# Two output projections, recast from half-by-half products into seven quadrant products

## The chip, the cores and the metric

The kernel runs on one core of a Trainium2 chip. Its time is the device time of one execution in microseconds. The change is timed against the kernel before it.

## The reference, cut to what matters

The program is a trunk of two layers over x of 1024 tokens by 1024 channels, in float32. The first layer is a gated DeltaNet (8 heads, keys of 128, values of 256, chunks of 64 in the reference), the second a sliding-window attention with sinks (32 query heads of 64, 4 key heads, window 128). Each layer ends in the same way: a gated output o of 1024 x 2048 is multiplied by a weight of 2048 x 1024 and added to the residual stream.

```
x = x + gated_deltanet_mixer(rms_norm(x, a_norm), ...)   # ... o (1024, 2048) @ a_w_out (2048, 1024)
k_band, v_band = shared_kv(x, kv_norm, w_kv, k_gain)
x = x + swa_sink_mixer(rms_norm(x, b_norm), ...)         # ... o (1024, 2048) @ b_w_out (2048, 1024)
```

These two matrix products are what the change is about.

## The kernel before

Float32 accuracy is had from TensorE with pairs: every operand is kept as a rounded high part (hi, oh, hh) and the rest (lo, ol, hl), and a product is three matmuls, high by high, high by low, low by high, accumulated in PSUM.

**Weights.** `weights()` is a generator that yields all weight pieces of the program in the order of use, each of 128 partitions x 1024 columns. `fetch()` takes the next piece: `weight_load` allocates a `wraw` tile (a pool of two buffers) and issues the load on SP's queue; then the high part is cast (on GpSimd where no gain is applied, L148; on ScalarE behind a multiplication by the gain on GpSimd, L150 and L151) and VectorE subtracts it for the low part (L152). `take()` hands out the oldest prepared weight and fetches until `depth` weights are ready. The pools from which hi and lo come rotate in `wpools`: in the first projection three buffers with a depth of 2, in the second two buffers with a depth of 1.

**The DeltaNet layer.** `layer_a` works head by head. `interleave` alternates the recurrence of one head (`head_delta`, a chain of small matmuls, VectorE and ScalarE steps) with the input projections of the next head (`head_in`, `head_z`, through `gemm_ct`, L175 to L179, 512 columns a matmul); TensorE's order is written out by that alternation and kept as it is, while the other engines' instructions are ordered by a scheduler. `head_out` writes the gated, transposed output of a head to `ogT` in DRAM (16 tiles of 128 channels x 1024 tokens). Head 7 comes last, and with it the z products of the two `late` heads.

**The attention layer.** `layer_b` does the same with `b_attend` (32 heads in 8 groups) and the q and z projections (`b_q`, `b_z`); its gated output goes to `og2` in DRAM.

**A projection.** `out_proj` goes over two halves of 512 tokens. In each half it goes over two pairs of 256 output columns; in each pair over four groups k4 of 512 input channels and the two column blocks b, with one weight tile each ([4, 256] per partition); for each weight tile over four blocks of 128 tokens and four channel blocks kk, three matmuls of 256 columns each (L913 to L915). Four PSUM tiles are accumulated over all of k4 and then added to the residual tiles `xo` (L919) and stored. The tokens' operand is held whole for a half: four pairs oh, ol of [128, 4, 512], loaded by `og_load` (a load of 512 KB on ScalarE's queue, a cast on ScalarE at L888, a subtraction on VectorE at L889, twice a pair). The second half's pairs replace the first's during the last column pair of the first half. After a half, `finish` normalizes the tokens and transposes them into `hT` for what follows (first projection only); `later` and `tick` place those transposes between matmuls.

Of the kernel before, what the change touches and what calls it, by code (L numbers as in the profile page):

```python
# [18 lines left out]
P = 128  # L19
# [45 lines left out]
class Kernel:  # L65
# [72 lines left out]
    def weight(self, src, shape, gain=None):  # L138
# [8 lines left out]
        if gain is None:  # L147
# [7 lines left out]
    def fetch(self):  # L155

        nxt = next(self.sources, None)
        if nxt is not None:
            self.ready.append(self.weight(*nxt))

# [90 lines left out]
    def layer_a(self):  # L251
        nc, tc, I = self.nc, self.tc, self.I
        with ExitStack() as ctx:
# [76 lines left out]
            for h in range(AH):  # L330
                cur = self.cur
                back = []
# [4 lines left out]
                if h + 1 == AH:  # L337
                    back += [self.head_z(i, None) for i in late]
                    self.first = self.og_tiles(self.dl0, "kq", "vt")
                    self.og_load(self.ogT, 0, 0, self.first, self.raws)  # L340
# [550 lines left out]
    def out_proj(self, og, resid, cur, tiles, raws, px, acc, dst, finish):  # L891


        nc = self.nc
        for half in range(2):
            xs, nxt = [], []
            for cp in range(2):
                cs = slice(cp * 512, cp * 512 + 512)
                ps = [acc.tile([P, 2, 256], F32, name="acc") for _ in range(4)]
                for k4 in range(4):  # L900
                    oh, ol = cur[k4]
                    for b in range(2):
                        hi, lo = self.take()
                        if cp == 0 and (k4, b) == (2, 0):
                            self.flush()
                            for c in range(4):
                                xs.append(px.tile([P, D], F32, name="xo", bufs=4))
                                nc.sync.dma_start(xs[c], resid[half * 4 + c])
                        for c in range(4):
                            ts = slice(c * P, c * P + P)  # L910
                            po = ps[c][:, b, :]
                            for kk in range(4):
                                nc.tensor.matmul(po, oh[:, kk, ts], hi[:, kk, :], start=(k4 + kk + b == 0), stop=False)  # L913
                                nc.tensor.matmul(po, oh[:, kk, ts], lo[:, kk, :], start=False, stop=False)  # L914
                                nc.tensor.matmul(po, ol[:, kk, ts], hi[:, kk, :], start=False, stop=(k4 + kk + b == 7))  # L915
                                if kk % 2:
                                    self.tick()
                            if (k4, b) == (3, 1):
                                nc.vector.tensor_tensor(out=xs[c][:, cs], in0=ps[c].rearrange("p b c -> p (b c)"),  # L919
                                                        in1=xs[c][:, cs], op=ALU.add)  # L920
                                nc.sync.dma_start(dst[half * 4 + c][:, cs], xs[c][:, cs])
                    if half == 0 and cp == 1:
                        nxt.append(tiles(k4))
                        self.og_load(og, 1, k4, nxt[-1], raws)
            cur = nxt
            finish(half, xs)
# [97 lines left out]
    def layer_b(self, last):  # L1024
# [4 lines left out]
        X = self.groups  # L1029
        X[0].keys, steps = self.key_stack(0)  # L1030
# [14 lines left out]
        def ahead():  # L1045
            for k4 in range(3):
                self.og_load(self.og2, 0, k4, last[k4], raws)
                yield 0.0
# [3 lines left out]
        self.og_load(self.og2, 0, 3, last[3], raws)  # L1052
# [198 lines left out]
    def run(self):  # L1251
        nc, tc, I = self.nc, self.tc, self.I
        with ExitStack() as ctx:
# [12 lines left out]
            self.late = (5, 6)  # L1266
            self.win = I["a_w_in"].rearrange("o (k p) c -> p (o k) c", p=P)
# [4 lines left out]
            with ExitStack() as c1:  # L1272
                hp = pool(c1, "hT")
                self.hT = self.hT_tiles(hp)
                with ExitStack() as c2:
# [23 lines left out]
                    def tiles(k4):  # L1299
                        return self.og_tiles(po, f"oh{k4}", f"ol{k4}") if k4 else self.og_tiles(self.dl0, "kq", "vt")  # L1300

                    cur = [self.first]
                    for k4 in range(1, 4):
                        cur.append(tiles(k4))
                        self.og_load(self.ogT, 0, k4, cur[-1], self.raws)
                    self.out_proj(self.ogT, xv, cur, tiles, self.raws, px, acc, x1d, finish)
# [21 lines left out]
                with ExitStack() as c2:  # L1328
                    px = pool(c2, "px2", 2)
                    self.out_proj(self.og2, x1d, last, lambda k4: last[k4],  # L1330
                                  lambda j: px.tile([P, 2, 512], F32, name="oraw"), px, pool(c2, "acc2", 6, space=PSUM), ov,
                                  lambda half, xs: None)

    def weights(self):
# [17 lines left out]
        for _ in range(2):  # L1352
            for c in (0, 2):
                for k in range(4):
                    for b in range(2):
                        yield four(rows("a_w_out"), k, c + b, None)
# [10 lines left out]
        for _ in range(2):  # L1367
            for c in (0, 2):
                for k in range(4):
                    for b in range(2):  # L1370
# [25 lines left out]
```

## Time and profile before

| | |
|---|---|
| time, median of 3 executions | 1904.08 us (1901.43 to 1906.32) |
| the profiled execution | 1903.49 us, its span 1901.7 us |
| TensorE, VectorE, ScalarE, GpSimd busy | 1831.0, 1232.2, 813.6, 517.1 us |
| DeltaNet layer after its start, to its last head's end | 100 to 903 us of the span |
| first output projection | 906.06 to 1095.27 us |
| keys and values, attention layer | 1095 to 1713 us |
| second output projection | 1713.34 to 1897.75 us |

A time here is that of one profiled execution; positions are counted from its first instruction. Records of TensorE's matmuls overlap, since one begins before the record of the one before it has ended; so the spacing of their starts tells the pace, and the duration of one does not. "PEld" is the load of the stationary operand.

### The profile page before, as it was taken

How to read it: one execution, taken by the hardware profiler on the slowest of the kernel's cores; microseconds unless marked ns; L12 is line 12 of the kernel's file. 1: busy time of each engine (PE TensorE's matmuls, PEld its weight loads, DVE VectorE, ACT ScalarE, POOL GpSimd, SP SyncE). 2: the span in 40 equal slices, each digit the busy share in tenths (PEclk: the TensorE clock that was granted, in tenths of full speed). 3: DMA queues.
4: the chain of work that ended last, by engine and by line, in shares of the span. 5: the costliest groups of instructions: out<-in, count | busy, mean ns of one | idle time of the engine just before them, and what ended most of it. 6: DMA issues, size and time to landing. Idle time of an engine off the chain costs nothing.

```text
span 1901.7 us, 33658 instructions
## 1 busy us (share of the span) xinstructions
PE 1831.0 (96%) x13186; PEld 1566.8 (82%) x13186; DVE 1232.2 (65%) x2868; ACT 813.6 (43%) x1948; POOL 517.1 (27%) x545
## 2 busy tenths in 40 slices
PE   6999999999999998999999999999999999999999
PEld 6677777787878776778999998888788788879999
DVE  6677766768585878765445266787786686753432
ACT  6446353535334353523112043557756656771100
POOL 0332222323232223220211222333433333321111
PEclk9999999999999999999999999999999999999999
DMA  4611111111111111122654321111201111226542
GB/s 148 148 37 39 55 35 56 34 56 45 34 57 34 57 34 57 34 84 95 233 181 153 112 89 45 45 30 51 67 29 51 56 40 51 73 73 196 185 172 80
DMA packets 151267, 149.72 MB, mean 79 GB/s; under 512 B 7242, under 2 KB 124484, under 8 KB 151108
## 3 DMA queue, kind: packets, MB, share of 16 engines
q1 hardware_dynamic: 140768, 130.40, 22.0%
q10 hardware_dynamic: 10340, 17.16, 2.8%
q8 instruction: 104, 1.70, 0.4%
q14 instruction: 55, 0.45, 0.1%
HBM read 116.05 MB, written 31.49 MB: 78 GB/s over the span
## 4 chain that ended last, share of the span: by engine, by line
PE 59%; DVE 20%; issue 8%; ACT 6%; POOL 5%; DMA 1%; SPq 0%; POOLq 0%; ACTq 0%; DVEq 0%
PE mm L177 6%; PE mm L175 6%; PE mm L179 6%; PE acc L914 6%; PE acc L913 6%; PE acc L915 6%; DVE acc L489 4%; PE mm L965 3%; PE mm L967 3%; PE mm L966 3%; DVE wlo L152 2%; ACT lsb L1176 2%; PE pv L1207 1%; POOL acc L486 1%; PE sc L796 1%
## 5 line engine op out<-in xcount | busy, mean ns | idle before, releaser
L175 PE MATMUL mm<-hh,whi 128*128 128x512 f32 (+1 forms) x1040 | 427.2, 411 | 2.3 <-ACT hh L241 2.2
L177 PE MATMUL mm<-hl,whi 128*128 128x512 f32 (+1 forms) x1040 | 417.5, 401 | 1.5 <-DVE hl L242 1.5
L179 PE MATMUL mm<-hh,wlo 128*128 128x512 f32 (+1 forms) x1040 | 415.2, 399 | 0.0
L152 DVE TENSOR_TENSOR wlo<-wraw,whi 128x1024 fp32r<-128x1024 f32 x146 | 184.2, 1262 | 245.7 <-POOL whi L148 219.4
L148 POOL TENSOR_SCALAR whi<-wraw 128x1024 fp32r<-128x1024 f32 x110 | 120.3, 1094 | 504.9 <-PE acc L915 246.4
L175 PEld LDWEIGHTS mm<-hh,whi 128*128 128x128 f32 x1040 | 197.6, 190 | 37.5 <-issue 5.0
L179 PEld LDWEIGHTS mm<-hh,wlo 128*128 128x128 f32 x1040 | 197.2, 190 | 36.2 <-issue 4.2
L177 PEld LDWEIGHTS mm<-hl,whi 128*128 128x128 f32 x1040 | 197.6, 190 | 34.4 <-issue 4.2
L965 PE MATMUL mm<-whi,hh 128*128 128x256 f32 x608 | 180.1, 296 | 0.0
L489 DVE SCALAR_TENSOR_TENSOR acc<-u,cw,acc 128x512 f32<-128x512 f32 x192 | 163.3, 853 | 23.9 <-POOL acc L486 21.8
L967 PE MATMUL mm<-whi,hl 128*128 128x256 f32 x608 | 171.9, 283 | 0.0
L966 PE MATMUL mm<-wlo,hh 128*128 128x256 f32 x608 | 171.8, 283 | 0.0
L913 PE MATMUL acc<-whi,hh 128*128 128x256 f32 x512 | 145.0, 283 | 0.0
L914 PE MATMUL acc<-wlo,hh 128*128 128x256 f32 x512 | 144.9, 283 | 0.0
L915 PE MATMUL acc<-whi,hl 128*128 128x256 f32 x512 | 144.9, 283 | 0.0
L1176 ACT ACTIVATE lsb<-lsb,nm 128x128 f32<-128x128 f32 x256 | 99.8, 392 | 64.2 <-DVE se L1172 54.9
L965 PEld LDWEIGHTS mm<-whi,hh 128*128 128x128 f32 x608 | 115.8, 190 | 11.0 <-issue 10.8
L966 PEld LDWEIGHTS mm<-wlo,hh 128*128 128x128 f32 x608 | 115.9, 191 | 0.2
L967 PEld LDWEIGHTS mm<-whi,hl 128*128 128x128 f32 x608 | 115.6, 190 | 0.0
L486 POOL TENSOR_SCALAR acc<-u,cw 128x512 f32<-128x512 f32 x64 | 63.0, 984 | 181.2 <-ACT u L482 166.8
L1180 POOL TENSOR_TENSOR lsb<-lsb,den 128x512 f32<-128x512 f32 x64 | 68.5, 1070 | 152.6 <-ACT pT L1190 51.5
L914 PE MATMUL acc<-wlo,oh 128*128 128x256 f32 x384 | 108.6, 283 | 0.0
(354 smaller groups left out, 4285.1 us busy)
## 6 DMA issues: line engine op xcount, KB each, us to landing
wraw<-in_a_w_in SPq DMA_DIRECT2D x48, 512.0 KB, 3.9
wraw<-in_a_w_out SPq DMA_DIRECT2D x32, 512.0 KB, 3.7
wraw<-in_b_w_in SPq DMA_DIRECT2D x32, 512.0 KB, 4.0
wraw<-in_b_w_out SPq DMA_DIRECT2D x32, 512.0 KB, 3.7
og<-zs SPq DMA_DIRECT2D x32, 256.0 KB, 2.0
ogT<-zs SPq DMA_DIRECT2D x24, 256.0 KB, 2.1
btab<-lt SPq DMA_DIRECT2D x1, 4096.0 KB, 24.1
dm<-gd SPq DMA_DIRECT2D x8, 512.0 KB, 3.6
```

Of the source, the lines that this page charges most:

```text
L152: nc.vector.tensor_tensor(out=lo, in0=raw, in1=self.f32(hi), op=ALU.subtract)
L175: nc.tensor.matmul(ps, hi[:, k, :], hh[:, k, :], start=(k == 0), stop=False)
L177: nc.tensor.matmul(ps, hi[:, k, :], hl[:, k, :], start=False, stop=False)
L179: nc.tensor.matmul(ps, lo[:, k, :], hh[:, k, :], start=False, stop=(k == KT - 1))
L489: nc.vector.scalar_tensor_tensor(out=acc, in0=u[:, t:t + 512], scalar=cw[:, t, blk:blk + 1], in1=acc, op0=ALU.mult, op1=ALU.add)
L913: nc.tensor.matmul(po, oh[:, kk, ts], hi[:, kk, :], start=(k4 + kk + b == 0), stop=False)
L914: nc.tensor.matmul(po, oh[:, kk, ts], lo[:, kk, :], start=False, stop=False)
L915: nc.tensor.matmul(po, ol[:, kk, ts], hi[:, kk, :], start=False, stop=(k4 + kk + b == 7))
L965: nc.tensor.matmul(ps, hh[:, k, ts], hi[:, k % 4, :], start=(k == 0), stop=False)
L966: nc.tensor.matmul(ps, hh[:, k, ts], lo[:, k % 4, :], start=False, stop=False)
L967: nc.tensor.matmul(ps, hl[:, k, ts], hi[:, k % 4, :], start=False, stop=(k == KT - 1))
L1176: nc.scalar.activation(out=L[:, e, :], in_=L[:, e, :], func=AF.Exp, bias=nm[:, e:e + 1], accum_out=den[:, e:e + 1])
```

## The change

With the two halves of the tokens, of the input channels and of the output columns, each projection is a product of 2 x 2 quadrants (o: tokens by channels; w: channels by columns). Instead of eight quadrant products it makes seven, after Strassen: each is the product of a quadrant, or a sum or difference of two, of o, with a quadrant or such a sum of w, and its result is added to or subtracted from one or two quadrants of the output. `PRODUCTS` lists them as (terms of o), (terms of w), (where the result goes, with sign).

- Five of the seven need a sum of two weight quadrants. `product_sums` forms these ahead of time, piece by piece (40 pieces of 128 x 512 a projection): two loads into a `wraw` tile, an addition on GpSimd, a store to `sums` in DRAM. One step is done at each `fetch()` (`self.side`): for the first projection in the DeltaNet layer from head 0 on, with what is left done ahead of head 7; for the second from the start of the attention layer, and on into the projection as far as needed.
- A weight tile is now [2, 512] per partition; its high part is cast on ScalarE (`second=True`).
- The tokens' operand passes through a ring of three pairs (first projection) or four (second), each for half a product (four channel blocks). `load` brings a quadrant into `whole` buffers (parts of hT that are free by then, in the first projection; three tiles `room` in the second), forms the sum on GpSimd where there are two terms, and splits it.
- All eight residual tiles are held from the start and loaded in quarters during the first two products. At the end of each product its PSUM tiles are added to or subtracted from them on VectorE; a quarter is stored when its last term has come. `finish` comes for the first half of the tokens after the sixth product, for the second half after the seventh.

```diff
+    PRODUCTS = (
+        (((1, 0, 0),), ((1, 0, 1), (-1, 1, 1)), ((0, 1, 1), (1, 1, 1))),
+        (((1, 1, 0), (-1, 0, 0)), ((1, 0, 0), (1, 0, 1)), ((1, 1, 1),)),
+        (((1, 1, 0), (1, 1, 1)), ((1, 0, 0),), ((1, 0, 1), (1, 1, -1))),
+        (((1, 0, 0), (1, 1, 1)), ((1, 0, 0), (1, 1, 1)), ((0, 0, 1), (1, 1, 1))),
+        (((1, 0, 0), (1, 0, 1)), ((1, 1, 1),), ((0, 0, -1), (0, 1, 1))),
+        (((1, 1, 1),), ((1, 1, 0), (-1, 0, 0)), ((1, 0, 1), (0, 0, 1))),
+        (((1, 0, 1), (-1, 1, 1)), ((1, 1, 0), (1, 1, 1)), ((0, 0, 1),)),
+    )
...
     def weight(self, src, shape, gain=None, second=False):
...
+        if second:
+            nc.scalar.copy(out=hi, in_=raw)
+        elif gain is None:
...
     def fetch(self):
...
             self.ready.append(self.weight(*nxt))
+            if self.side is not None:
+                next(self.side, None)
...
+    def product_sums(self, w, sums):
...
+            for i in range(8):
+                t = self.wraw.tile([P, 2, 512], F32, name="wraw")
+                for j, (_, k, c) in enumerate(terms):
+                    nc.sync.dma_start(t[:, j, :], w[:, 8 * k + i, 512 * c:512 * c + 512])
+                nc.gpsimd.tensor_tensor(out=t[:, 0, :], in0=t[:, 0, :], in1=t[:, 1, :],
+                                        op=ALU.add if terms[1][0] > 0 else ALU.subtract)
+                yield
+                nc.sync.dma_start(sums[n, i], t[:, 0, :])
...
+    def out_proj(self, og, resid, ring, ready, raws, whole, px, acc, dst, finish):
...
+        def load(u):
+            terms = self.PRODUCTS[u // 2][0]
+            oh, ol = ring[u % len(ring)]
+            src = [quadrant(t, k, u % 2) for _, t, k in terms]
+            for j in range(2):
+                js = slice(2 * j, 2 * j + 2)
+                if len(src) == 1:
+                    raw = src[0][:, js, :]
+                else:
+                    raw = raws(j)
+                    nc.gpsimd.tensor_tensor(out=raw, in0=src[0][:, js, :], in1=src[1][:, js, :],
+                                            op=ALU.add if terms[1][0] > 0 else ALU.subtract)
+                nc.scalar.copy(out=oh[:, js, :], in_=raw)
+                nc.vector.tensor_tensor(out=ol[:, js, :], in0=raw, in1=self.f32(oh[:, js, :]), op=ALU.subtract)
...
+        for m, (_, _, sinks) in enumerate(self.PRODUCTS):
+            ps = [acc.tile([P, 512], F32, name="acc") for _ in range(4)]
+            for j in range(4):
+                hi, lo = self.take()
+                if (m, j) == (0, 3):
+                    self.flush()
+                if m < 2 and j in (1, 2):
+                    for c in range(4):
+                        tc.keep_in_program_order(nc.sync.dma_start(xs[j - 1][c][:, 512 * (1 - m):1024 - 512 * m],
+                                                                   resid[(2 - j) * 4 + c][:, 512 * (1 - m):1024 - 512 * m]))
+                oh, ol = ring[(2 * m + j // 2) % len(ring)]
+                for c in range(4):
+                    ts = slice(c * P, c * P + P)
+                    for kk in range(2):
+                        k = 2 * (j % 2) + kk
+                        nc.tensor.matmul(ps[c], oh[:, k, ts], hi[:, kk, :], start=(j + kk == 0), stop=False)
+                        nc.tensor.matmul(ps[c], oh[:, k, ts], lo[:, kk, :], start=False, stop=False)
+                        nc.tensor.matmul(ps[c], ol[:, k, ts], hi[:, kk, :], start=False, stop=(j == 3 and kk == 1))
+                        self.tick()
+                    if j == 3:
+                        for t, q, sign in sinks:
+                            x = xs[t][c][:, 512 * q:512 * q + 512]
...
+                            if left[t, q] == 1:
+                                nc.sync.dma_start(dst[(1 - t) * 4 + c][:, 512 * q:512 * q + 512], x)
+                if j % 2 and 2 * m + j // 2 + len(ring) < 14:
+                    load(2 * m + j // 2 + len(ring))
...
+                if h == 0:
+                    self.side = self.product_sums(self.rows("a_w_out"), self.sums[0])
+                elif h + 1 == AH:
+                    for _ in self.side:
+                        pass
+                    self.side = None
```

## Rows read from the trace of the kernel before

**Rows 1.** The page: span, busy time of each engine, TensorE's granted clock in 40 slices.
```profile
span 1901.7 us, 33658 instructions
PE 1831.0 (96%) x13186; PEld 1566.8 (82%) x13186; DVE 1232.2 (65%) x2868; ACT 813.6 (43%) x1948; POOL 517.1 (27%) x545
...
PEclk9999999999999999999999999999999999999999
```

**Rows 2.** Busy time in four stages: layer, projection, layer, projection.
```profile
core 0: us, PE busy (x) PEld busy (x) DVE busy (x) ACT busy (x) POOL busy (x), PEclk, DMA share, GB/s
100.00:903.36 803.36, 767.98 (x5375) 609.29 (x5373) 582.95 (x1104) 339.94 (x794) 217.74 (x231) 0.99 0.16 49
906.06:1095.27 189.21, 188.04 (x1571) 187.83 (x1570) 79.52 (x90) 25.91 (x35) 39.70 (x34) 1.00 0.52 171
1120.00:1712.00 592.00, 580.19 (x4050) 493.86 (x4048) 420.29 (x1412) 364.10 (x968) 200.26 (x218) 0.99 0.16 51
1713.34:1897.75 184.41, 184.41 (x1538) 184.36 (x1536) 65.34 (x60) 13.95 (x15) 31.80 (x30) 1.00 0.48 160
```

**Rows 3.** What TensorE waited for, over the span, longest in total first.
```profile
PE sc L810 <- DVE lh L799: 8.3, 10, 1.9
...
PE tp L1186 <- POOL lsb L1180: 6.1, 5, 2.7
...
PE acc L914 <- DVE wlo L152: 1.2, 1, 1.2
```

**Rows 4.** Timeline of TensorE: first and last of the second projection's 1536 matmuls.
```profile
1713.34 0.38 PE L913 MATMUL acc<-whi,hh 128*128 128x256 f32 x1
...
1897.63 0.28 PE L915 MATMUL acc<-whi,hl 128*128 128x256 f32 x1
```

**Rows 5.** Timeline of TensorE: first and last of 23 consecutive 512-column matmuls.
```profile
898.10 0.39 PE L177 MATMUL mm<-hl,whi 128*128 128x512 f32 x1
...
903.09 0.39 PE L179 MATMUL mm<-hh,wlo 128*128 128x512 f32 x1
```

**Rows 6.** Groups of instructions by form, second projection (the cast on ScalarE: first).
```profile
L151 ACT CAST whi<-wraw 128x1024 fp32r<-128x1024 f32 x2 | 2.1, 1047 | 63.9 <-PE acc L915 63.9
...
L152 DVE TENSOR_TENSOR wlo<-wraw,whi 128x1024 fp32r<-128x1024 f32 x30 | 36.7, 1224 | 95.8 <-POOL whi L148 95.8
L148 POOL TENSOR_SCALAR whi<-wraw 128x1024 fp32r<-128x1024 f32 x30 | 31.8, 1060 | 148.0 <-PE acc L915 133.9 <-DMA wraw<-in_b_w_out 14.1
L889 DVE TENSOR_TENSOR hl<-oraw,hh 128x1024 fp32r<-128x1024 f32 x8 | 11.9, 1526 | 10.9 <-ACT hh L888 10.9
L919 DVE TENSOR_TENSOR xo<-acc,xo 128x512 f32<-128x512 f32 x15 | 10.1, 690 | 10.8 <-PE acc L915 10.8
```

**Rows 7.** DMA issues by line: count, size, median us from issue to landing.
```profile
wraw<-in_b_w_out SPq DMA_DIRECT2D x32, 512.0 KB, 3.7
og<-zs SPq DMA_DIRECT2D x32, 256.0 KB, 2.0
...
xo<-x1d SPq DMA_DIRECT2D x8, 512.0 KB, 7.2
```

**Rows 8.** Busy time in a stretch at the first projection's start (columns as above).
```profile
920.00:925.00 5.00, 5.00 (x44) 5.00 (x43) 2.76 (x3) 0.96 (x1) 2.10 (x1) 1.00 1.06 384
```

**Rows 9.** Timeline at the change of half, second projection: start, us, engine.
```profile
1770.39 2.00 ACT L888 CAST hh<-oraw 128x1024 fp32r<-128x1024 f32 x2 [46.02 <-PE acc L914]
...
1771.46 3.07 DVE L889 TENSOR_TENSOR hl<-oraw,hh 128x1024 fp32r<-128x1024 f32 x2 [3.64 <-ACT hh L888]
1774.46 1.21 DVE L152 TENSOR_TENSOR wlo<-wraw,whi 128x1024 fp32r<-128x1024 f32 x1
```

**Rows 10.** GpSimd's groups in the attention layer; two instructions of the first projection.
```profile
L1180 POOL TENSOR_TENSOR lsb<-lsb,den 128x512 f32<-128x512 f32 x64 | 68.5, 1070 | 152.6 <-ACT pT L1190 51.5 <-DVE den L1179 49.2 <-ACT zs L1108 19.1
L150 POOL TENSOR_TENSOR wraw<-wraw,gcolb 128x1024 f32<-128x1024 f32 x32 | 67.4, 2109 | 80.2 <-DMA wraw<-in_b_w_in 46.3 <-DVE sskb L981 7.3 <-DVE rkbt L118 5.2
...
908.97 2.06 DVE L889 TENSOR_TENSOR ol<-kt,oh 128x1024 fp32r<-128x1024 f32 x1
...
921.03 2.10 POOL L148 TENSOR_SCALAR whi<-wraw 128x1024 fp32r<-128x1024 f32 x1 [6.82 <-DMA wraw<-in_a_w_out]
```

More of the change, by code (lines that the diff above doesn't have):

```diff
@@ L136, in weight_first, with weight @@
         self.ready.append((hi, lo))
-    def weight(self, src, shape, gain=None):
+    def weight(self, src, shape, gain=None, second=False):
         nc = self.nc
@@ L889, in og_load @@
             nc.vector.tensor_tensor(out=ol[:, js, :], in0=raw, in1=self.f32(oh[:, js, :]), op=ALU.subtract)
-    def out_proj(self, og, resid, cur, tiles, raws, px, acc, dst, finish):
-        nc = self.nc
[L895 to L926, printed above, removed]
@@ L1029, in layer_b @@
         X = self.groups
+        self.side = self.product_sums(self.rows("b_w_out"), self.sums[1])
         X[0].keys, steps = self.key_stack(0)
@@ L1045, in ahead @@
         def ahead():
-            for k4 in range(3):
-                self.og_load(self.og2, 0, k4, last[k4], raws)
+            for k4 in range(2):
+                self.og_load(self.og2, 1, k4, last[k4], raws)
                 yield 0.0
@@ L1051, in layer_b @@
         self.flush()
-        self.og_load(self.og2, 0, 3, last[3], raws)
     @staticmethod
@@ L1266, in run @@
             self.late = (5, 6)
+            self.sums = [dr.tile([5, 8, P, 512], F32, name=f"sums{i}") for i in range(2)]
+            self.rows = rows = lambda name: I[name].rearrange("o (k p) c -> p (o k) c", p=P)
+            self.side = None
             self.win = I["a_w_in"].rearrange("o (k p) c -> p (o k) c", p=P)
@@ L1297, in finish @@
                             self.later((15, 10)[half] + (2, .8)[half] * j, f)
[L1299 to L1306, printed above, removed]
+                    ring = [self.first] + [self.og_tiles(po, f"oh{i}", f"ol{i}") for i in range(2)]
+                    room = [self.hT[0][0], self.hT[1][0], self.hT[1][1]]
+                    self.out_proj(self.ogT, xv, ring, 1, self.raws, lambda i: self.f32(room[i]), px, acc, x1d, finish)
                     wk = [self.take(False), self.take(False)]
@@ L1329, in run @@
                     px = pool(c2, "px2", 2)
-                    self.out_proj(self.og2, x1d, last, lambda k4: last[k4],
-                                  lambda j: px.tile([P, 2, 512], F32, name="oraw"), px, pool(c2, "acc2", 6, space=PSUM), ov,
-                                  lambda half, xs: None)
+                    room = pool(c2, "room")
+                    self.out_proj(self.og2, x1d, last, 2, lambda j: px.tile([P, 2, 512], F32, name="oraw"),
+                                  lambda i: room.tile([P, KT, 512], F32, name=f"room{i}"), px,
+                                  pool(c2, "acc2", 6, space=PSUM), ov, lambda half, xs: None)
     def weights(self):
@@ L1351, in weights @@
                     yield col(self.win, b, None)
[L1352 to L1356, printed above, removed]
+        yield from self.product_weights(rows("a_w_out"), self.sums[0])
         wkv = I["w_kv"].rearrange("(k p) c -> p k c", p=P)
@@ L1366, in weights @@
                 yield col(bin_, 16 + 2 * hg + j, self.gcolb[:, 8:16])
[L1367 to L1370, printed above, removed]
-                        yield four(rows("b_w_out"), k, c + b, None)
+        yield from self.product_weights(rows("b_w_out"), self.sums[1])
     def dump(self, name, ap):
```

42 lines of the change are left out of this document (40 added, 2 removed).

## The prediction

> **What bounds the kernel now.** I read the page first: TensorE is busy for 96% of the span, VectorE for 65%, and the granted clock stays at the 2.4 GHz level nearly throughout [rows 1]. Busy time alone says little here, because the records of neighbouring matmuls overlap, so I went on to the view by stages. It splits the run into the DeltaNet layer, the first output projection, the attention layer and the second projection [rows 2]. The projections last 189.2 and 184.4 us, and the reader should note how idle the other engines are there: VectorE 79.5 and 65.3 us, GpSimd 39.7 and 31.8 us. Then the list of what TensorE waits for: the longest waits are those of the recurrence in the DeltaNet layer, then 6.1 us for GpSimd in the attention layer; in the projections only 1.2 us are waited for a weight's low part [rows 3]. So the projections are bound by TensorE's own instruction stream, and a change in that stream shows in full as long as its operands come in time.
>
> Next I need the step from one matmul to the next, not its duration. The second projection's first and last matmuls start 184.29 us apart with 1535 steps between them: 0.1201 us a step at 256 columns [rows 4]. An undisturbed stretch at 512 columns gives 22 steps in 4.99 us: 0.2268 us [rows 5].
>
> **Removed: matmuls.** A projection has 2 halves x 2 column pairs x 4 x 2 weight tiles x 4 row blocks x 4 x 3 = 1536 matmuls of 256 columns: 1536 x 0.1201 = 184.4 us. After: 7 products x 4 weight tiles x 4 row blocks x 2 x 3 = 672 of 512 columns: 672 x 0.2268 = 152.4 us. That is 32.0 us less each, 64.0 for both. An eighth of the work (23.0 us) is Strassen's; the other 9 come from the wider tile, since 0.2268 is less than two steps of 0.1201.
>
> The rows first: two narrow steps take 0.240 us, one wide step 0.2268 [rows 4, 5]. The Trainium skill (TensorE: Matmul & The Clock Gate, Back-to-back issue gap) gives an isolated gap of columns over the clock plus about 2.5 ns, so 109 ns and 216 ns; by that the saving would be 22.7 us a projection, 45.4 in all, where the rows give 64.0. Both rows stand above the page's figures, and the trace decides.
>
> The profiled execution took 1903.5 us, 1.8 more than its span, and 0.6 less than the median of 1904.1. Without any stall the change would give 1903.5 - 64.0 = 1839.5. What remains is what the operands cost.
>
> **The pace of weights.** A weight tile now serves 24 matmuls of 0.2268 us, 5.44 us, where it served 48 of 0.1201, 5.76 us. Its preparation is a load (3.7 us), a cast to the high part (1.06 us on GpSimd, now a cast on ScalarE of 1.05) and VectorE's subtraction (1.22) [rows 6, 7]. Per product of 21.8 us VectorE has four of these, four of the ring's subtractions (1.23 to 1.53) and on average 6.9 additions of 0.69 from PSUM: about 15.5 us. No engine is full; it is a question of order and lead.
>
> **First projection: +2.** Three weight buffers rotate and two weights are fetched ahead, so a late one has a spare period. The loads at the start are alike in size (quadrants and residual instead of tiles and residual); the transfers of that moment already ran at 384 GB/s [rows 8], and TensorE lost 1.2 us. Bounds: 0, and 8 us if the second product's quadrants (2 MB, with 2 MB of residual and the weights beside them) land one period and a half late.
>
> **Second projection, start: +12.** Counting fetches, the attention layer forms 32 of its 40 sums; the other 8 fall into the first nine fetches of the projection. While they do, they hold one of the two load buffers, so each weight must pass load, cast and subtraction in one buffer: 3.7 + 1.05 + 1.22 = 6.0 us against 5.44, 0.5 late, 5 us for nine weights. If loads land as late as the residual's in that stage (7.2 us [rows 7]), it is 9.5 against 5.44, 36 us. Zero is possible too, if the freed buffer alternates well. SP's queue is in order: behind a sum's store (2.0 us for such a size), which waits for GpSimd's addition, stand the next sum's loads, the residual's and the next weight's. I take 12, nearer the quiet end, since the residual is in flight for the first two products only.
>
> **Second projection, later: +6.** Here only one weight is fetched ahead. The nearest row is the change of half in the kernel before: ScalarE begins two casts at 1770.39, VectorE does two subtractions in 3.07 us, and only then the weight's, which ends at 1775.67, 5.3 us after the buffer came free [rows 9]. The old period of 5.76 covered that; the new one of 5.44 barely does. There are ten such reloads of the ring during the products now. In their way come GpSimd's sums of residual quadrants and, at a product's end, the last block's second pair of additions (1.4 us). A sum is some 1.0 us longer than the cast that lay there, the additions come on top, and 0.2 us are left of the period: between nothing and (1.0 + 1.4 - 0.2) x 10 = 22 us I take 0.6 each.
>
> What GpSimd does to VectorE is in the rows: one subtraction beside GpSimd's work took 2.06 us where another took 1.22, and a cast beside VectorE's work 2.10 instead of 1.06 [rows 6, 10]. The Trainium skill (SBUF — State Buffer, SBUF: two separate sides) states it as an exclusive lock: a VectorE operation with two SBUF inputs and a GpSimd one that reads SBUF do not share, the later one waits for the whole of the other. The trace agrees with that in size, so a sum of 2 us can delay a subtraction by up to 2 us.
>
> **The sums in the layers: +8.** 72 additions of 128x512 fall into the two layers; one of that form takes 1.07 us [rows 10]. Their cover is GpSimd's idle time (218 of 803 us busy, 200 of 592 [rows 2]). With no cover they would cost 72 x 1.07 = 77 us, with full cover nothing. The nearest row is the gain multiplication: 32 of 2.11 us in the attention layer [rows 10], and there TensorE's waits for GpSimd are 6.1 us in all [rows 3]. So I take 8, about 0.1 each. Their transfers (0.8 MB a sum, 31 MB a layer) add some 40 to 55 GB/s to 50 where the chip has moved 384 [rows 2, 8], and SP has some 20 us between weights in the first layer.
>
> Costed at nothing: the reload of the first quadrant, the drain of the last three sums ahead of head 7 (over 100 us before their use), the stores (the same bytes), the norms of both halves (as before: one behind the last product but one, one at the end), the tail.
>
> Sum: 1839.5 + 2 + 12 + 6 + 8 = 1867.5; against the median, 0.6 more: 1868.
>
> **Rivals.** (a) Everything is hidden, 1840 to 1849. For it: in the kernel before, the second projection ran without one wait. Against: the shorter period and shared buffers. (b) The second projection becomes paced by preparing weights, not by TensorE: at 6.6 us a weight (6.0 and a hand-over) 28 take 185 us, and its gain is gone; with the same layer cost, 1903.5 - 32.0 + 2 + 8 = 1882, up to 1897 with the loads late at its start. For it: one weight of lead, and [rows 9]. Against: only ten of 28 weights meet a ring load. (c) Slower: GpSimd's sums sit on the recurrence. Each holds a VectorE operation in the DeltaNet layer (583 of 803 us busy) or the softmax's chain, TensorE waits for it in its fixed order, and all 77 us are paid: 1903.5 - 64.0 + 77 = 1917. It decides from 64 / 72 = 0.9 us a sum on. For it: TensorE's longest waits are for VectorE there; against it, the gain multiplications. (d) A wide matmul costs two narrow ones in this place (0.240): 9 us less gained each, 1886. Against: every undisturbed step at 512 columns.
>
> **Chances.** My forecast (1850 to 1881) 0.54, (a) 0.19, (b) 0.15, (c) 0.06, (d) 0.03, anything else 0.03. The range takes the forecast, most of (a) and most of (b): 1843 to 1892. A measurement tells about 0.3%, 5.7 us. Faster by more: the forecast, (a), (d) and nearly all of (b), 0.89; within: 0.05; slower: 0.06. The forecast's own range is 1850 to 1881.
>
> **What would show it.** Right: wide matmuls of the products stepping at 0.227 us; first projection near 157 us, second 165 to 180; TensorE's new waits for weights' high and low parts, most of them in the first 60 us of the second projection; layers within 10 us of 803 and 592. Wrong: a step of 0.24, a projection waiting throughout, or TensorE waits for VectorE in the DeltaNet layer grown by tens of us. The prediction fails most easily in the second projection's start, which no row shows.

## The result, and the profile after

The changed kernel takes 1947.63 us (median of four runs, 1945.47 to 1954.68) where the kernel before takes 1904.62: a ratio of 1.0234, 95% interval 1.0205 to 1.0264. It is slower by 43 us; 1868 was forecast, with 1843 to 1892 as the range. The profiled execution took 1948.09 us with a span of 1946.4, against 1901.7 [rows 1].

The page of the kernel after: span, busy time of each engine, and TensorE's granted clock in the 40 slices.

```profile
span 1946.4 us, 30832 instructions
...
PE 1804.9 (93%) x11458; PEld 1468.5 (75%) x11458; DVE 1323.0 (68%) x2948; ACT 891.4 (46%) x2028; POOL 676.1 (35%) x601
...
PEclk9999999999999999999899999999999999997899
```

TensorE has less to do (1804.9 us instead of 1831.0), and its idle time has doubled, from 70.7 us of the span to 141.5. GpSimd gained 159 us of work, VectorE 91. The granted clock, level nearly throughout before, now drops in slice 20, where the first projection starts, and in slices 37 and 38, in the second. The view by stages of the kernel after, layer, projection, layer, projection, answers to [rows 2]:

```profile
core 0: us, PE busy (x) PEld busy (x) DVE busy (x) ACT busy (x) POOL busy (x), PEclk, DMA share, GB/s
100.00:925.40 825.40, 777.44 (x5387) 616.61 (x5385) 592.07 (x1104) 340.79 (x795) 277.93 (x270) 0.98 0.27 88
927.68:1095.91 168.23, 164.09 (x708) 132.37 (x707) 123.19 (x130) 65.75 (x74) 68.39 (x24) 0.97 0.52 178
1120.00:1742.00 622.00, 587.75 (x4049) 497.74 (x4049) 423.54 (x1414) 364.90 (x972) 241.30 (x249) 0.99 0.29 92
1743.64:1942.33 198.69, 166.66 (x674) 132.24 (x672) 102.83 (x100) 52.55 (x53) 65.54 (x27) 0.91 0.52 176
```

The first projection is 21.0 us shorter, the second 14.3 longer. The edges of the projections give the rest: the first starts at 927.68 instead of 906.06 (+21.6), and from its end to the second's start there are 647.7 us instead of 618.1 (+29.6). So -21.0 + 14.3 + 21.6 + 29.6 = +44.5, the change of span (44.7). Both layers became longer, and the second projection paid too. Of the 52.0 us by which the two layers' windows grew, 35.0 are idle time of TensorE (12.6 and 22.4); in the other 17 it is busy longer with nearly the same matmuls, in part at the lower clock (0.98 instead of 0.99 in the DeltaNet layer). VectorE's instructions there, the same in number or nearly so, are busy only 9.1 and 3.3 us longer. The list of TensorE's waits in the kernel after (us in total, times, longest), beside [rows 3]:

```profile
PE tp L1275 <- POOL lsb L1269: 24.8, 17, 2.9
PE acc L997 <- ACT whi L148: 20.3, 7, 9.6
PE acc L998 <- DVE wlo L154: 15.9, 10, 4.1
PE sc L820 <- DVE lh L809: 11.2, 10, 2.9
```

The wait for GpSimd's normalised scores rose from 6.1 to 24.8 us: that is the attention layer. In the DeltaNet layer it is VectorE that TensorE waits longer for, in many small waits: 34.7 us in all instead of 22.1. The waits for weights rose from 1.2 to 36.2, nearly all in the second projection. VectorE's largest wait from the first projection's end to the second's start, before and then after:

```profile
DVE qh L1133 <- POOL qh L1131: 39.4, 40, 4.1
```

```profile
DVE qh L1222 <- POOL qh L1220: 84.9, 45, 7.4
```

GpSimd's group of 80 sums of weight quadrants, over the span (busy, mean ns, idle before them and what ended it):

```profile
L938 POOL TENSOR_TENSOR wraw<-wraw 128x512 f32<-128x512 f32 x80 | 115.9, 1448 | 178.7 <-DMA wraw<-in_a_w_out 99.4 <-DMA wraw<-in_b_w_out 45.8 <-DVE lh L809 10.2
```

One addition takes 1.45 us, not the 1.07 of [rows 10], and GpSimd stood 178.7 us in front of them, 145 of it because their loads had not landed.

The timeline of TensorE around the second projection's longest stall:

```profile
1749.68 0.39 PE L999 MATMUL acc<-whi,hl 128*128 128x512 f32 x1
...
1754.44 0.39 PE L999 MATMUL acc<-whi,hl 128*128 128x512 f32 x1
1764.45 0.79 PE L997 MATMUL acc<-whi,hh 128*128 128x512 f32 x1 [9.62 <-ACT whi L148]
1765.90 0.80 PE L998 MATMUL acc<-wlo,hh 128*128 128x512 f32 x1 [0.66 <-DVE wlo L154]
1766.49 0.63 PE L999 MATMUL acc<-whi,hl 128*128 128x512 f32 x1
1766.92 0.63 PE L997 MATMUL acc<-whi,hh 128*128 128x512 f32 x1
```

Ahead of the stall 21 steps take 4.76 us, 0.2267 each: the matmuls step as forecast. Then nothing for 10.0 us, because ScalarE's cast of a weight comes late, and behind the stall the step is 0.43 us, the lower of the clock's two levels (1.2 GHz), for eleven steps, 2.2 us more. What ScalarE and GpSimd did meanwhile, from the same kernel's timelines of the two engines:

```profile
1746.73 1.49 ACTq L960 DMA_DIRECT2D room<-og  x3
1760.11 1.04 ACT L975 CAST hh<-oraw 128x1024 fp32r<-128x1024 f32 x1 [14.92 <-POOL oraw L973]
1762.41 1.04 ACT L975 CAST hh<-oraw 128x1024 fp32r<-128x1024 f32 x1 [1.26 <-POOL oraw L973]
...
1763.36 1.04 ACT L148 CAST whi<-wraw 128x1024 fp32r<-128x1024 f32 x1
```

```profile
1757.74 4.64 POOL L973 TENSOR_TENSOR oraw<-room,room 128x1024 f32<-128x1024 f32 x2 [19.76 <-DMA room<-og]
```

The quadrants of `og` are asked for at 1746.73; GpSimd can add them at 1757.74; ScalarE, which works in order, stands in front of the ring's cast for 14.9 us; and the weight's cast, on which TensorE waits, is queued behind it.

### The profile page after: what moved, and what is told of

It is laid out like the page before. It is cut to its first block, busy times and chain, and to the rows that moved or that the text cites. A ratio compares the mean times of both kernels' runs of the same rounds, so it can differ in the third digit from the quotient of the medians.

```text
span 1946.4 us, 30832 instructions
## 1 busy us (share of the span) xinstructions
PE 1804.9 (93%) x11458; PEld 1468.5 (75%) x11458; DVE 1323.0 (68%) x2948; ACT 891.4 (46%) x2028; POOL 676.1 (35%) x601
## 4 chain that ended last, share of the span: by engine, by line
PE 44%; DVE 23%; DMA 10%; POOL 9%; issue 7%; ACT 5%; SPq 0%; POOLq 0%; ACTq 0%; DVEq 0%
PE mm L181 5%; PE mm L179 5%; PE mm L183 5%; PE acc L998 4%; PE acc L999 4%; DVE acc L499 4%; PE acc L997 4%; DVE wlo L154 3%; DMA wraw<-in_b_w_in 3%; DMA wraw<-in_b_w_out 2%; POOL wraw L938 2%; DMA sums<-wraw 2%; ACT lsb L1265 2%; PE sc L806 1%; PE mm L1054 1%
## 5 line engine op out<-in xcount | busy, mean ns | idle before, releaser
L938 POOL TENSOR_TENSOR wraw<-wraw 128x512 f32<-128x512 f32 x80 | 115.9, 1448 | 178.7 <-DMA wraw<-in_a_w_out 99.4
L152 POOL TENSOR_TENSOR wraw<-wraw,gcolb 128x1024 f32<-128x1024 f32 x36 | 72.0, 2001 | 159.8 <-DMA wraw<-in_b_w_in 101.4
L150 POOL TENSOR_SCALAR whi<-wraw 128x1024 fp32r<-128x1024 f32 x46 | 50.6, 1100 | 204.0 <-PE mm L181 186.5
L997 PE MATMUL acc<-whi,hh 128*128 128x512 f32 x224 | 92.1, 411 | 19.8 <-ACT whi L148 19.8
L998 PE MATMUL acc<-wlo,hh 128*128 128x512 f32 x224 | 92.2, 412 | 12.2 <-DVE wlo L154 12.2
```

The source lines that it names most:

```text
L938: nc.gpsimd.tensor_tensor(out=t[:, 0, :], in0=t[:, 0, :], in1=t[:, 1, :], op=ALU.add if terms[1][0] > 0 else ALU.subtract)
L997: nc.tensor.matmul(ps[c], oh[:, k, ts], hi[:, kk, :], start=(j + kk == 0), stop=False)
L998: nc.tensor.matmul(ps[c], oh[:, k, ts], lo[:, kk, :], start=False, stop=False)
```

## The experiments

Each run is compared with the kernel before on the same chip. The table has, from each profiled execution, where the first projection starts, its length, the time from its end to the second's start (keys, values, attention), and the second's length. The layers differ by up to some 7 us between profiles even where nothing in them is changed (first starts of e1 and e8, 904.2 and 911.0; z1's 622.9 between, 618.1 before), so only larger differences are read from single profiles. In e1 and e8 TensorE's idle time in the DeltaNet layer is the same, 37.7 and 37.2 us; the granted clock is not, 1.00 and 0.99.

| run | median us | ratio, 95% interval | start of 1st | 1st | between | 2nd |
|---|---|---|---|---|---|---|
| before | 1904.1 | | 906.1 | 189.2 | 618.1 | 184.4 |
| after | 1947.6 | 1.0205 to 1.0264 | 927.7 | 168.2 | 647.7 | 198.7 |
| e1 no sums | 1881.1 | 0.9866 to 0.9902 | 904.2 | 168.5 | 619.0 | 182.4 |
| e3 transfers without additions | 1887.7 | 0.9902 to 0.9931 | 907.7 | 167.9 | 613.5 | 193.4 |
| e5 additions without transfers | 1926.2 | 1.0097 to 1.0143 | 931.7 | 168.7 | 636.3 | 182.0 |
| e6 memset for each addition | 1891.2 | 0.9916 to 0.9956 | 911.5 | 168.6 | 622.7 | 181.8 |
| e2 addition a fetch later, order fixed | 2010.1 | 1.0543 to 1.0577 | 953.0 | 167.3 | 673.6 | 209.3 |
| e8 e1, ring behind the weight | 1871.2 | 0.9811 to 0.9844 | 911.0 | 163.8 | 618.3 | 171.7 |
| e9 after, ring behind the weight | 1941.6 | 1.0166 to 1.0221 | 925.6 | 165.7 | 650.3 | 196.4 |
| e10 e9, sums done in the layer | 1929.4 | 1.0095 to 1.0157 | 928.7 | 167.0 | 665.5 | 170.3 |
| e11 e10, sums on VectorE | 1892.8 | 0.9914 to 0.9962 | 922.3 | 166.6 | 626.9 | 171.6 |
| e12 e11, a fetch later | 1887.4 | 0.9893 to 0.9926 | 921.2 | 165.5 | 620.8 | 172.2 |
| e13 e12, sums on GpSimd | 1932.1 | 1.0112 to 1.0175 | 926.4 | 166.0 | 658.4 | 172.3 |
| z1 eight products, 512 columns | 1892.5 | 0.9923 to 0.9956 | 906.5 | 183.1 | 622.9 | 174.2 |

**e1.** Where a product needs a sum of weight quadrants, it takes the first quadrant alone, and no sums are formed.

```diff
-                if len(terms) == 1:
+                if len(terms) >= 1:
...
-        self.side = self.product_sums(...)
+        self.side = iter(())
```

> Leaves out the sums of weight quadrants: no loads, additions or stores for them, and a product that needs a sum takes its first quadrant alone, so that the same bytes are loaded and the same matmuls run. All three theories of the layers' loss (1: GpSimd's queue stands still in front of an addition whose loads have not landed; 2: the additions themselves hold VectorE; 3: the transfers and the load buffers that they share with the weights) expect the two layers to lose nothing any more: the first projection begins at 906 us of the span as before the change (928 after it), the attention layer with keys and values takes 618 (648). It tells how much of the second projection's 199 us is due to the sums: 165 or less if nearly all of its stalls are, 185 or more if the order on ScalarE and the sums of residual quadrants are what holds it. Time 1867 to 1890.

The sums are the loss: without them 1881.1. Both layers are back at their old lengths (904.2 and 619.0 against 906.1 and 618.1), so the sums cost 23.4 + 28.7 = 52 us in the layers, and 16 in the second projection, which takes 182.4 even so. (e8 has no sums either; against its layers the loss is 46.)

**e3.** Loads, stores and their buffers as in the change, the addition left out.

```diff
-                nc.gpsimd.tensor_tensor(out=t[:, 0, :], in0=t[:, 0, :], in1=t[:, 1, :], op=...)
```

> Leaves out the additions alone: the loads of both quadrants and the store of the first stay, with their buffers and their queue. Theories 1 and 2 expect the layers' loss to fall below 10 us, time near 1895. Theory 3 expects it to stay at some 50 us, time near 1945.

The 31 MB a layer cost nothing that shows in the layers (907.7, 613.5). The second projection keeps 11 of its 16 us.

**e5.** The reverse: the additions on GpSimd, from a resident tile into the same buffers, with no load and no store; weights as in e1.

```diff
-                    nc.sync.dma_start(t[:, j, :], w[...])
-                nc.gpsimd.tensor_tensor(out=t[:, 0, :], in0=t[:, 0, :], in1=t[:, 1, :], op=...)
+                c = self.cst[:, 0:256].unsqueeze(1).broadcast_to([P, 2, 256])
+                nc.gpsimd.tensor_tensor(out=t[:, 0, :].rearrange("p (a b) -> p a b", a=2), in0=c, in1=c, op=...)
...
-                nc.sync.dma_start(sums[n, i], t[:, 0, :])
```

> The additions alone, on data that is already in SBUF, with no loads and no stores; a product that needs a sum takes its first quadrant. Theory 2 expects most of the layers' 51 us to stay. Theory 1 expects 10 us or less, since GpSimd has nothing to stand in front of; theory 3 nothing. The second projection should be as without any sums.

27.5 + 17.3 = 45 us in the layers, 0.6 us for each of the 73 that the trace has there (40 and 33; the other 7 fall into the second projection). The additions carry the price, not their traffic.

**e6.** As e5, with a write of about the same length in place of the addition.

```diff
-                nc.gpsimd.tensor_tensor(out=t[:, 0, :].rearrange("p (a b) -> p a b", a=2), in0=c, in1=c, op=...)
+                nc.gpsimd.memset(t, 0.0)
```

> As the additions alone, but GpSimd fills the tile with zeros (about as long, some 1.0 us) where it added: it writes SBUF and reads nothing. A product that needs a sum takes its first quadrant; nothing is loaded or stored for sums. If an addition costs by holding VectorE's operations with two SBUF inputs (theory 2), the layers lose less than 8 us against the run without any sums, time near 1885. If it costs by GpSimd's own queue being that much later, the layers lose the same 45 us as with additions, time near 1925.

7.3 + 3.7 = 11 us; the medians of e6 and e1 say 10. The groups of the two kernels: GpSimd's added instruction over the span, e5 first, then e6.

```profile
L937 POOL TENSOR_TENSOR wraw<-cst 128x512 f32<-128x512 f32 x80 | 94.1, 1178 | 84.5 <-DVE wlo L154 63.5 <-DVE sso L834 10.5 <-DVE nm L1257 8.5
```

```profile
L936 POOL MEMSET wraw<- 128x1024 f32 x80 | 76.2, 952 | 85.2 <-DVE wlo L154 84.2 <-POOL wraw L936 0.9
```

And VectorE's convolution taps in the DeltaNet layer (100 to 900 us), e5 first, then e6:

```profile
L499 DVE SCALAR_TENSOR_TENSOR acc<-u,cw,acc 128x512 f32<-128x512 f32 x168 | 155.1, 923 | 19.5 <-POOL acc L496 17.5
```

```profile
L499 DVE SCALAR_TENSOR_TENSOR acc<-u,cw,acc 128x512 f32<-128x512 f32 x168 | 143.2, 852 | 20.0 <-POOL acc L496 18.1
```

GpSimd is occupied for 94 us in the one and 76 in the other, and stands equally long in front of them (84.5 and 85.2), yet the cost is four times as large. With additions that read SBUF a tap took 923 ns in the mean, with the writes 852, and TensorE's waits for VectorE in that layer were 42.2 and 28.4 us in all (24.5 in e1). So most of e5's cost isn't GpSimd's occupied time, which is a fifth shorter in e6, but comes with the reading of SBUF. In the change itself the taps took 872 ns, hardly more than the 851 before.

**e2.** The addition of the change one fetch behind its loads, ahead of the next weight's cast, its order fixed, so that GpSimd doesn't stand in front of loads.

```diff
+    def sum_store(self, t, sign, dst):
+        tc.keep_in_program_order(nc.gpsimd.tensor_tensor(out=t[:, 0, :], in0=t[:, 0, :], in1=t[:, 1, :], op=...))
+        nc.sync.dma_start(dst, t[:, 0, :])
```

> The same sums, but each is added and stored one fetch after its loads were issued, behind the work that GpSimd has been given up to then, so that GpSimd never stands in front of a load. Theory 1 expects most of the layers' 51 us back: less than 15 left, time near 1905. Theory 2 expects them to stay (the same 72 additions), time 1940 to 1950. Theory 3 the same or more, since a sum now holds its load buffer longer.

A clear miss for theories 1 and 2: 2010.1, both layers 26 us longer than in the change, though GpSimd no longer stood in front of any addition in the layers. Theory 3 allowed for it, but in e3 the same transfers cost the layers nothing that shows. The order of GpSimd's work and the time for which a load buffer is held changed together, so the run doesn't say which of them cost it, nor what the standing alone costs.

**e8 and e9.** The loads of the ring's quadrants (of the tokens' operand) stay where they were issued; their sums, casts and subtractions go behind the next weight's, the casts and subtractions in fixed order. e8 does so to e1, e9 to the whole change.

```diff
-                if j % 2 and 2 * m + j // 2 + len(ring) < 14:
-                    load(2 * m + j // 2 + len(ring))
+                    wait.append((u, bring(u)))
...
+                if wait and m + j:
+                    load(*wait.pop(0))
```

> As the run without sums (a product that needs a sum takes its first quadrant), but in both projections a ring slot's casts and subtractions are traced behind the next weight's and kept there on ScalarE and VectorE; the loads of the quadrants stay where they were. If the second projection's stalls come from the weight's high part standing in ScalarE's queue behind a ring cast that waits for GpSimd's sum and its loads, the second projection falls from 182 us to 165 or less and the time to 1865 or less. If they come from GpSimd's sums holding VectorE, or from late loads, it stays within 5 us of 182.

> The whole change with the same order in the projections, sums of weights and all. The layers should lose their 51 us as before; the second projection should fall from 199 us to 175 to 185, if the order is its main cost, and the time to 1925 to 1935. If its main cost is the nine weights that share load buffers with the last sums, it stays above 190.

Without sums the second projection falls from 182.4 to 171.7 us and the first from 168.5 to 163.8: the ring in front of a weight on ScalarE cost some 11 us there. That is between the two theories' lengths (165 or less, within 5 of 182), so the order was a part. With the sums it is only 198.7 to 196.4, so something that comes with the sums stands in front.

**z1.** The kernel before with eight products and no sums, only the weight tiles of 2x512 instead of 4x256, so that its matmuls have 512 columns.

```diff
-                ps = [acc.tile([P, 2, 256], F32, name="acc") for _ in range(4)]
+                ps = [acc.tile([P, 512], F32, name="acc") for _ in range(4)]
...
-                            for kk in range(4):
+                            for kk in range(2):
+                                k = 2 * b + kk
```

> The kernel before with nothing changed but the shape of the projections' weight tiles: two channel blocks by 512 columns instead of four by 256, so that each matmul has 512 columns; eight quadrants' worth of work, no sums. 768 matmuls of 0.2268 us are 174.2 us a projection where 1536 of 0.1201 are 184.4: 10 us less each, time near 1884, with no change in the layers. If weights come too late at a period of 5.44 us even here, the projections keep 180 us or more, time above 1893.

The first and last matmul of its second projection:

```profile
1712.46 0.50 PE L914 MATMUL acc<-whi,hh 128*128 128x512 f32 x1
...
1886.47 0.39 PE L916 MATMUL acc<-whi,hl 128*128 128x512 f32 x1
```

767 steps in 174.01 us, 0.2269 each, with no stall. 10 us of the 32 forecast for a projection need no Strassen, and this kernel is 11.5 us faster than the one before. About 20 were expected: its first projection fell by 6 us only, to 183.1, and the undisturbed steps there take 0.2317 us in the mean. The Trainium skill (TensorE: Matmul & The Clock Gate, Back-to-back issue gap) gives 216 ns for an isolated matmul of 512 columns, by which this projection would take 166 us, an estimate; the trace's step is 227 ns.

**e10.** e9, and every third fetch of the attention layer advances the sums by two steps, so that all forty are done before the second projection.

```diff
                 next(self.side, None)
+                self.steps += 1
+                if self.more and self.steps % 3 == 0:
+                    next(self.side, None)
```

> The whole change with the quarters' casts behind the next weight (as in e9), and the second layer's sums formed at a rate of four in three fetches, so that all forty are done before the second projection starts. Theory (what keeps the second projection at 196.4 us are the nine last sums: their loads and stores take the buffers that the weights are loaded into, and GpSimd forms them between the residual's quarters): its length falls to 165 to 176 us, near the 171.7 us of the run without sums. Rival (the loads of the sums, stored in DRAM, or GpSimd's sums of quarters set it): it stays at 185 to 198 us. The stretch of keys, values and attention holds nine more sums; at 0.3 to 1.1 us each it lengthens from 650 to 653 to 660 us. Median by the theory 1922 to 1932 us, by the rival 1942 to 1952 us.

The second projection falls to 170.3 us, as the theory of the last sums has it (seven additions by the trace, not nine). The attention layer is 15.2 us longer for them, above the 3 to 10 that were expected; the profiled execution was the slowest of four, 7.9 us above their median, so a part may be its own.

**e12, e13 and e11.** The last question was whether it is the engine. e12 puts e10's additions on VectorE, one fetch behind their loads; e13 is the same with the additions back on GpSimd; e11 has them on VectorE right behind the issue of their loads.

```diff
-                nc.gpsimd.tensor_tensor(out=t[:, 0, :], in0=t[:, 0, :], in1=t[:, 1, :], op=...)
                 yield
+                nc.vector.tensor_tensor(out=t[:, 0, :], in0=t[:, 0, :], in1=t[:, 1, :], op=...)
                 nc.sync.dma_start(sums[n, i], t[:, 0, :])
```

> As e10, but the 80 additions of weight quadrants run on VectorE instead of GpSimd, each one fetch after its loads were issued, so that it doesn't stand in front of them. Theory (the sums cost some 0.6 us each in the layers because GpSimd's addition holds VectorE's two-input operations back): VectorE now pays each addition as an operation of its own, at some 0.6 to 0.7 us (half of a weight's low part of 128x1024, 1.22 us), and a part of these falls into its idle time; the layers cost 15 to 40 us over the kernel without sums instead of 52, and with the projection as in e10 the median is 1890 to 1920 us. Rival (what the sums cost is their place in the queues and the traffic of their transfers, not the engine): layers at 45 us or more, median as e10's or above it.

> As e12, with the additions back on GpSimd and everything else as there, so that the two differ by the engine of the 80 additions alone. Theory (the engine: GpSimd's addition holds VectorE's operations back): the layers cost 35 to 55 us over the kernel without sums instead of 19, median 1905 to 1935 us. Rival (e12 gained by putting the addition one fetch behind its loads): the layers stay below 28 us, median 1885 to 1900 us.

> As e12, with the additions on VectorE right behind their own loads' issue instead of one fetch later. If the place matters, VectorE stands in front of loads that have not landed (GpSimd stood 207 us in front of its 80 in e10), everything behind it stands too, and the layers cost 35 us or more, median above 1905 us; if only the engine matters, 1885 to 1897 us.

e12 is faster than both kernels, 1887.4 us, 0.9909 of the one before. e13, which differs from it by the engine of 80 instructions alone, takes 1932.1. Against e1 the layers cost 17.0 + 1.8 = 18.8 us in e12 and 22.1 + 39.4 = 61.5 in e13, which is more than the 35 to 55 expected. e8 has the projections' order of these two, and against it the layers cost 10.2 + 2.5 = 12.7 and 15.4 + 40.1 = 55.5; the medians, each against its kernel before, give 14 and 60 for the whole kernel. Nearly all of the difference lies in the attention layer. The groups in the stretch from the first projection's end to the second's start, e12's additions and VectorE's low parts of the queries:

```profile
L1236 DVE TENSOR_TENSOR qh<-qr,qh 128x256 fp32r<-128x256 f32 x64 | 30.3, 474 | 42.8 <-POOL qh L1234 42.6
L942 DVE TENSOR_TENSOR wraw<-wraw 128x512 f32<-128x512 f32 x40 | 28.3, 708 | 24.6 <-DMA wraw<-in_b_w_out 23.8 <-issue 0.6
```

The same two groups of e13:

```profile
L942 POOL TENSOR_TENSOR wraw<-wraw 128x512 f32<-128x512 f32 x40 | 54.9, 1373 | 75.0 <-DMA wraw<-in_b_w_out 75.0
L1236 DVE TENSOR_TENSOR qh<-qr,qh 128x256 fp32r<-128x256 f32 x64 | 39.4, 617 | 80.6 <-POOL qh L1234 80.5
```

With GpSimd's additions VectorE's operation is longer (617 ns, 474) and starts later (80.5 us of waiting for GpSimd, 42.6), because GpSimd's queue is later: 10 of its 64 high parts of queries come directly behind an addition, and 23.5 of the 80.5 us belong to these. How much of the rest was passed on from an addition further ahead, or from its loads, isn't shown. TensorE's waits for GpSimd's scores, e12 and then e13:

```profile
PE tp L1289 <- POOL lsb L1283: 7.5, 6, 3.0
```

```profile
PE tp L1289 <- POOL lsb L1283: 25.9, 19, 3.0
```

How one addition holds VectorE, from e13's timelines of VectorE and GpSimd:

```profile
1364.87 1.26 DVE L1273 TENSOR_SCALAR nm<-m 128x4 f32<-128x4 f32 x1
1366.04 0.15 DVE L1275 TENSOR_TENSOR se<-sink,m 128x4 f32<-128x4 f32 x1
...
1523.76 1.50 DVE L1236 TENSOR_TENSOR qh<-qr,qh 128x256 fp32r<-128x256 f32 x1 [3.27 <-POOL qh L1234]
```

```profile
1364.35 1.74 POOL L942 TENSOR_TENSOR wraw<-wraw 128x512 f32<-128x512 f32 x1
...
1523.68 1.30 POOL L942 TENSOR_TENSOR wraw<-wraw 128x512 f32<-128x512 f32 x1
```

The second addition runs from 1523.68 to 1524.98; the operation that VectorE starts 0.08 us after it takes 1.50 us, of which the last 0.28 lie behind the addition's end. Beside the first addition an operation of 128x4, as small as the one of 0.15 us behind it, takes 1.26 us and ends with the addition, at 1366.1. The Trainium skill (SBUF — State Buffer, SBUF: two separate sides) has this as an exclusive lock: a VectorE operation with two SBUF inputs and a GpSimd one that reads SBUF, or a VectorE one in a two-port mode and any GpSimd one, don't run together, and the later waits for the whole of the other. The second addition's row agrees, and so does e6, whose writes cost a quarter; in which mode the operation of 128x4 ran no row shows.

e12's layers lie in the range expected of them, its median a little below. e11's 1892.8 lies where the engine alone decides; standing in front of fresh loads on VectorE costs 5 to 7 us of median and no more.

## Why the prediction was wrong, by its own steps

**Matmuls, -64.0: right but for 3 us.** Steps of 0.2267 us in the second projection of the change; in z1's and after each stall's recovery the same. In the first projection the undisturbed steps take 0.2318 us in the mean, which gives back 3.4 us of its 32; why, no run shows. Rival (d), with 0.240, falls.

**The step that failed: the sums in the layers, +8.** They cost 52 us against e1 (51 against before, 46 against e8), some 0.7 each instead of 0.1. The prediction took GpSimd's idle time for their cover. Idle time of the adding engine was not what counted: an addition can hold a VectorE operation until it ends, and in the attention layer GpSimd is itself a link of the softmax chain, so what stands in its queue delays the link. The prediction had read the first from its own rows, a subtraction of 2.06 us beside GpSimd's work, and put no price on it in the layers. The nearest row chosen, the gain multiplications with 6.1 us of TensorE's waits, showed what a load already there cost, not what the next addition would. It is rival (c)'s place for the loss, given 0.06, at some 0.7 us a sum; but its sign, TensorE's waits for VectorE in the DeltaNet layer grown by tens of us, did not come (34.7 for 22.1). Rival (c) was to decide only from 0.9 us on, but that bound supposed both projections' gains whole.

How the 45 to 61 us of GpSimd's additions divide is shown in part. e6 puts occupancy and standing in front of buffers at some 11 us, for an instruction a fifth shorter; up to 34 of e5's 45 us come with the read. In the change VectorE itself was held for little: its operations are busy 12.4 us longer in the two layers, beside 104 us of additions there, and in the attention layer, where the loss is larger, only 3.3 of these. There the time shows as waits for GpSimd, TensorE's 24.8 us instead of 6.1 and VectorE's 84.9 instead of 39.4. In the attention layer the change costs 11 us more than e5, which lies in the loads that GpSimd stands in front of or in longer additions; no run tells those apart. In the DeltaNet layer the engine matters little (15.4 and 10.2 against e8 in e13 and e12): with the additions on VectorE it has 40 more operations there, and TensorE's idle time in that layer is 8 us longer in e12 than in e8.

**Second projection, +18 (start 12, later 6): 46.3.** 198.7 is 152.4 and 46.3. The first part was too small: with the last sums out of the stage (seven by the trace, eight by the prediction's count), 196.4 falls to 170.3, 26 us (bounds 0 to 36). That it lies with their loads, stores and buffers, as the prediction had it, is supported by e3, which keeps 193.4 without any addition, and e5, which has 182.0 without transfers; buffers, queue and traffic weren't told apart. The ring in front of weights cost 10.7 in e8 against 6 (bounds 0 to 22), but moving it gave 2.3 with the sums there, and the low clock behind each long stall, which the sum didn't have, is part of both: 37 steps of 0.43, 7.5 us. 18 us remain in e10, nearly all in its first 43 us. The longest single stall is neither term as costed: the ring's first quadrants land 11 us after they were asked for, GpSimd adds them then, and the weight's cast stands behind the ring's; e1, without sums of weights, has it too (12.5 us from 1702.58). What the prediction calls sums of residual quadrants there are sums of the tokens' operand. Rival (b), 185 us from weight preparation, is about the length that e1 and e5 then have (182), but as a few stalls, not as a slower pace.

**First projection, +2: 11.** The stage lost 21.0 us and not 32. The slower steps are 3.4 of the 11; TensorE stood 4.2 us at 935.5 for a low part behind three of the ring's subtractions, and 19 steps ran at the lower clock, 3.8 us more. It became 163.8 in e8; forecast was near 157.

**The sum.** -64 + 11 + 46.3 + 51.2 = +44.5, where -64 + 2 + 18 + 8 was forecast. Of the 80 us between, 43 are the layers', 28 the second projection's, 9 the first's.

## What to carry to other kernels

Before work is given to an idle GpSimd, look at what VectorE does at that time and at which links of the critical chain GpSimd holds itself. Additions that read SBUF held VectorE here, and in order they delayed GpSimd's own links; the same additions on VectorE cost the layers 13 us in place of 56 (against e8), although VectorE was the busier engine. A step that only saves TensorE instructions in one stage should be costed by what it adds to the stages that feed it, and split where it can be: the wider tile alone gave 11.5 us, and of the 20 us by which e12's projections are shorter than z1's its sums took some 12 (against their kernels before, e12 gains 18.8 us and z1 11.5). In a queue that is worked in order, what has to be waited for goes behind what is needed next (the ring behind the weight, 11 us).

## What the runs showed that was not expected

A stall costs more than its length: behind the 10.0 us at 1754.44 TensorE's steps were 0.43 us instead of 0.2267 eleven times, and the granted clock of the stage fell to 0.91, where z1's, without a stall, is 1.00. The same happened behind the stall of 4.2 us in the first projection, again for eleven steps.

GpSimd's addition of 128x512 is no fixed price either: 1.07 us in the kernel before [rows 10], 1.18 alone in e5, 1.41 and 1.45 in e13 and the change. VectorE's takes 0.71 us in the attention layer and 0.89 in the DeltaNet layer, by e12's groups.
